# Forget sums of the keys: from TensorE products to rows read back from DRAM and added with the masks

## The chip, the core and the metric

The kernel runs on one core of one Trainium2 chip. Its engines are TensorE (PE, with its weight loads shown apart as PEld), VectorE (DVE), ScalarE (ACT), GpSimd (POOL) and SyncE (SP), which here only issues transfers. Times are device microseconds (us) of the whole program. Three runs of the kernel before took 1853.32, 1856.33 and 1856.56 us, so their median is 1856.33 us.

## The reference

One step of a two-layer network on 256 prompt rows and 8 streams of 16 sample rows (384 rows in all, three blocks of 128). Layer 0 has eight "fox" heads, softmax attention with a forget gate, and eight stick-breaking heads. Layer 1 is a gated MLP. The change touches the scores of the fox heads alone:

```python
F = cumsum(log_sigmoid(f_logit))                     # one forget sum per row and head
s = einsum('bqhd,bkhd->bhqk', q, k) * ATTN_SCALE
s = s + (Fq[..., :, None] - Fk[..., None, :])        # query's sum minus key's sum
s = where(kpos <= qpos, s, -inf)
p = softmax(s)
```

For a score matrix with queries on the partitions, `Fq` is one number per partition, and `-Fk` is one row that is the same for all partitions. The sample rows also attend to 128 cached keys per stream, whose sums run over the cached gates.

## The kernel before

All weights arrive in units of 256 KB (128 x 512 floats) that SP loads. Each unit is split into a rounded part `whi` (ACT, line 79) and a rest `wlo` (DVE, line 81); three products per block (lines 102 to 104, or 118 to 120) then give the result of one layer's projection in PSUM. `whi` and `wlo` have four buffers each, `raw` five, so a unit can be prepared about three units ahead of its use. The tiles named `d` are the PSUM banks of the projections (four), the tiles named `a` those of everything else (four).

Layer 0 starts with the transposes of x (line 162), then the keys of the first two heads (`first`), the row sums of squares (lines 204 and 207), their inverse root `rstd`, and `rstd_bc`, the same over all partitions, made by a product of a diagonal matrix `rdiag` with ones (line 147) and copied out by ACT (line 148). The values of the first heads come from `values_first` (lines 359 to 361), which also computes the forget logits.

`forget` then makes the sums. `FT` (8 heads x 384 rows) holds the sums of prompt and sample rows; `Fnat` holds the same with rows on partitions. The negated sums of the keys are kept in three tiles in the split form that TensorE's rounded type needs (heads on partitions 0 to 7 the rounded part, 32 to 39 the rest): `nFP` for prompt queries, `nFS` for the sample block, `nFc` for the cached keys. `E_all` picks one head out of these partitions for all 128 output partitions, and `selD` gives each group of 16 partitions its own stream's row.

`pair(g)` handles two heads. For g from 0 to 3 these are fox heads, for 4 to 7 stick-breaking heads. It projects keys, values, queries and gates, writes the keys back (`natural`), and loads the cached keys and values through POOL's queue (lines 420 and 422). `head` computes one head: `KT` by transposes on DVE (line 454), scores `sc` (prompt) and `sd` (sample) on TensorE, `z` = scores + `Fnat` + mask on DVE (line 481), the maximum, the exponential, and the products with the values.

The order of the instructions on each engine is fixed when the program is built: a scheduler runs the program text through a timing model and lets each engine take what that model says is ready. Every engine then works strictly in that order. A change of one instruction's modelled time can therefore move others.

Of the kernel before, what the change touches and what calls it, by code (L numbers as in the profile page):

```python
# [8 lines left out]
F32 = mybir.dt.float32  # L9
# [27 lines left out]
def tile_hybrid_step(  # L37
# [129 lines left out]
    with ExitStack() as l0:  # L167
# [44 lines left out]
        def late():  # L212
            es = ExitStack()
            for i in done[-1]:
                es.enter_context(tc.issue_after(i.ins))
            return es


        def select(ap, pattern, base, cm, fill=0.0, op=ALU.is_ge):
            G.affine_select(out=ap, in_=ap, pattern=pattern, compare_op=op, fill=fill, base=base, channel_multiplier=cm)  # L220
# [33 lines left out]
            select(mdn, [[-16, 8], [-1, 16]], -strict, 1, NEG)  # L254
            masks.append((mp, md))

        selD_f = lp.tile([P, P], F32, tag="os", name="selD_f")
        V.memset(selD_f, 0.0)
        sel8 = lp.tile([8, P], F32, tag="os", name="sel8")
        V.memset(sel8, 1.0)  # L260
        select(sel8, [[1, P]], 0, -16)
        select(sel8, [[-1, P]], 15, 16)
        selD = lc.tile([P, P], F32R, name="selD")
        with late():
            S.activation(selD_f[0:8], sel8, AF.Copy)
            S.activation(selD_f[32:40], sel8, AF.Copy)
            S.activation(selD, selD_f, AF.Copy)
        E_f = lc.tile([P, 8], F32, name="E_f")
        V.memset(E_f, 0.0)
        E_all = lc.tile([P, 8], F32R, name="E_all")  # L270
        with late():
            S.activation(E_f[0:8], ident[0:8, 0:8], AF.Copy)
            S.activation(E_f[32:40], ident[0:8, 0:8], AF.Copy)
            S.activation(E_all, E_f, AF.Copy)


        wf = lc.tile([P, KT, 8], F32, name="wf")
        bfg = lc.tile([P, 8], F32, name="bfg")
        clf = lc.tile([P, 8, 8], F32, name="clf")
        Fnat = lc.tile([P, NT, 8], F32, name="Fnat")  # L280
        nFP = lc.tile([P, T], F32R, name="nFP")
        nFS = lc.tile([P, T], F32R, name="nFS")
        nFc = lc.tile([P, 8, P], F32R, name="nFc")
        logf = lc.tile([P, NT, 8], F32, name="logf")

        V.tensor_copy(wf[:, 0, 0:1], hlo[1][:, 3, 0:1].bitcast(F32))
# [5 lines left out]
        def forget(o):  # L292
            gains(1)
            z = lc.tile([P, NT, 8], F32, name="fz")
            for tb in range(NT):
                V.scalar_tensor_tensor(out=z[:, tb, :], in0=o[tb][:, 256:264], scalar=rstd[:, tb:tb + 1], in1=bfg, op0=ALU.mult, op1=ALU.add)
            e = lc.tile([P, NT, 8], F32, name="fe")
            S.activation(e, z, AF.Abs)
            S.activation(e, e, AF.Exp, scale=-1.0)
            S.activation(e, e, AF.Ln, bias=1.0)  # L300
            V.scalar_tensor_tensor(out=logf, in0=z, scalar=0.0, in1=e, op0=ALU.min, op1=ALU.subtract)
            G.dma_start(flf_p.rearrange("o (t p) h -> p (o t) h", p=P), logf[:, :2, :])
            G.dma_start(flf_s.rearrange("b q h -> (b q) h"), logf[:, 2, :])

            b3 = bank()
            PE.matmul(b3[:8, :2 * P], lhsT=logf[:, 0, :], rhs=UT, start=True, stop=False)
            PE.matmul(b3[:8, P:2 * P], lhsT=logf[:, 1, :], rhs=UT[:, :P], start=False, stop=True)
            bs = bank()
            PE.matmul(bs[:8, :P], lhsT=logf[:, 2, :], rhs=BT, start=True, stop=True)
            for b_ in range(8):  # L310
                PE.matmul(bs[:8, P + b_:P + b_ + 1], lhsT=clf[:, b_, :], rhs=ones[:, 0:1], start=True, stop=True)
            tot = lc.tile([8, 8], F32, name="ftot")
            V.tensor_copy(tot, bs[:8, P:P + 8])
            FT = lp.tile([8, T], F32, tag="PT", name="FT")
            V.tensor_copy(FT[:, :2 * P], b3[:8, :2 * P])
            V.tensor_tensor(out=FT[:, 2 * P:].rearrange("h (b q) -> h b q", q=16), in0=bs[:8, :P].rearrange("h (b q) -> h b q", q=16),
                            in1=tot.unsqueeze(2).broadcast_to([8, 8, 16]), op=ALU.add)
            b4 = bank()
            for tb in range(NT):
                PE.transpose(b4[:, tb * 8:(tb + 1) * 8], FT[:, tb * P:(tb + 1) * P], ident[:8, :8])  # L320
            V.tensor_copy(Fnat, b4[:, :24].rearrange("p (t h) -> p t h", h=8))
            for t in (nFP, nFS):
                S.activation(t, ones[:, 0:1].broadcast_to([P, T]), AF.Copy, scale=0.0)
            for t, o, n, f in ((nFP, 0, 2 * P, 0), (nFP, 2 * P, P, 0), (nFS, 2 * P, P, 2 * P)):
                S.activation(t[0:8, o:o + n], FT[:, f:f + n], AF.Copy, scale=-1.0)
                V.scalar_tensor_tensor(out=t[32:40, o:o + n], in0=FT[:, f:f + n], scalar=-1.0, in1=f32(t[0:8, o:o + n]), op0=ALU.mult, op1=ALU.subtract)
            for hg in range(2):
                b5 = bank()
                for hh in range(4):
                    PE.matmul(b5[:8, hh * P:(hh + 1) * P], lhsT=clf[:, :, 4 * hg + hh], rhs=UT[:, :P], start=True, stop=True)  # L330
                hs = slice(4 * hg, 4 * hg + 4)
                b5v = b5[:8].rearrange("b (h p) -> b h p", p=P)
                S.activation(nFc[:, hs, :], ones[:, 0:1].unsqueeze(2).broadcast_to([P, 4, P]), AF.Copy, scale=0.0)
                S.activation(nFc[0:8, hs, :], b5v, AF.Copy, scale=-1.0)
                V.scalar_tensor_tensor(out=nFc[32:40, hs, :], in0=b5v, scalar=-1.0, in1=f32(nFc[0:8, hs, :]), op0=ALU.mult, op1=ALU.subtract)

        mixhi, mixlo = [], []
        vprev = [None]
# [108 lines left out]
        def head(g, hh, h, kT, vn, qT, kc, vc):  # L447
            fox = g < 4
            mp, md = masks[0 if fox else 1]

            KTt = []
            for hf in range(2):
# [2 lines left out]
                KTt.append(t)  # L455

            sc = bank()
            E_h = E_all[:, h:h + 1].broadcast_to([P, P])
            if fox:
                PE.matmul(sc[:, :T], lhsT=E_h, rhs=nFP, start=True, stop=False)  # L460
            PE.matmul(sc[:, :2 * P], lhsT=qT[:, P:2 * P], rhs=kT[:, :2 * P], start=not fox, stop=not fox)
            PE.matmul(sc[:, 2 * P:T], lhsT=qT[:, :P], rhs=kT[:, :P], start=not fox, stop=True)
            sd = bank()
            if fox:
                PE.matmul(sd[:, :T], lhsT=E_h, rhs=nFS, start=True, stop=False)
                PE.matmul(sd[:, :2 * P], lhsT=selD, rhs=nFc[:, h, :].unsqueeze(1).broadcast_to([P, 2, P]), start=False, stop=False)
# [307 lines left out]
```

## Time and profile before

| | |
|---|---|
| runs | 1853.32, 1856.33, 1856.56 us; median 1856.33 |
| profiled execution | 1854.33 us, of which the span from first to last instruction is 1852.6 us |
| granted TensorE clock | 0.998 of full speed |
| busy: PE, PEld, DVE, ACT, POOL | 99%, 90%, 52%, 39%, 12% of the span |
| DMA | 268 MB, mean 145 GB/s |

A row of a timeline gives the start in us, the time in us, engine, line, operation, the tile written and the tiles read, the shape, and how many instructions were merged. In brackets stands idle time of the engine just before the row, and what ended it. A PE matmul's end is modelled, and one starts while the one before it still drains, so what a matmul costs the engine is the distance from its start to the next one's start, not its duration.

### The profile page before, as it was taken

The page shows a single profiled execution, that of the slowest core. Times are in us where ns is not written, and L with a number is a line of the kernel's source. Part 1 is how long each engine was busy: PE and PEld are TensorE (multiplying, and loading weights), DVE is VectorE, ACT ScalarE, POOL GpSimd, SP SyncE. Part 2 cuts the span into 40 slices and gives each one's busy share as a digit, 9 for nine tenths or more (in the row PEclk, how much of TensorE's full clock was granted, in tenths as well). Part 3 has the DMA queues.
Part 4 walks back from the last instruction along what each step waited for, and adds up shares of the span by engine and source line. Part 5 has one row for each costly group of instructions (what it writes and reads, how often), then busy time and mean ns, then how long its engine had stood idle before and what let it go on. Part 6 is the DMA issues. An engine that isn't in the chain of part 4 may idle for free.

```text
span 1852.6 us, 27262 instructions
## 1 busy us (share of the span) xinstructions
PE 1828.7 (99%) x10107; PEld 1674.4 (90%) x10107; DVE 961.1 (52%) x1671; ACT 720.0 (39%) x1281; POOL 223.4 (12%) x366
## 2 busy tenths in 40 slices
PE   8999999999999999999999999999999999999997
PEld 7999899899899877788888999989998899989986
DVE  6555355556546544543343654545544555445456
ACT  5344343444544543433333433333332333333334
POOL 2421213213212001310000100001000100000000
PEclk9999999999999999999999999999999999999999
DMA  5855556565656467744444454445444444444453
GB/s 174 189 158 131 166 135 161 146 165 142 160 147 155 129 172 196 226 137 126 135 126 127 139 144 125 118 126 161 126 127 120 142 147 126 121 126 146 127 150 123
DMA packets 208582, 268.42 MB, mean 145 GB/s; under 512 B 19424, under 2 KB 149648, under 8 KB 208320
## 3 DMA queue, kind: packets, MB, share of 16 engines
q1 hardware_dynamic: 185088, 226.03, 43.3%
q0 software_dynamic: 16160, 35.93, 8.0%
q10 hardware_dynamic: 7200, 4.72, 0.8%
q8 instruction: 79, 1.29, 0.3%
q14 instruction: 55, 0.45, 0.1%
HBM read 251.91 MB, written 14.69 MB: 144 GB/s over the span
## 4 chain that ended last, share of the span: by engine, by line
PE 56%; DMA 3%; issue 2%; DVE 1%; ACT 1%; POOL 1%; ACTq 0%; POOLq 0%; DVEq 0%
PE d L104 9%; PE d L103 9%; PE d L102 9%; PE d L119 9%; PE d L120 9%; PE d L118 9%; DMA blk<-h1d 2%; PE a L673 1%; DMA raw<-in_w_out_dram 1%; POOL blk L553 0%; DMA slot<-in_sgu_ln_g_dram 0%; DMA h1d<-slot 0%; DVE wlo L81 0%; ACT sq L722 0%; DVE slot L719 0%
## 5 line engine op out<-in xcount | busy, mean ns | idle before, releaser
L81 DVE TENSOR_TENSOR wlo<-raw,whi 128x512 fp32r<-128x512 f32 x800 | 547.3, 690 | 716.1 <-ACT whi L79 715.0
L79 ACT ACTIVATE whi<-raw 128x512 fp32r<-128x512 f32 x800 | 503.5, 631 | 930.5 <-PE d L103 492.3
L104 PE MATMUL d<-slot,wlo 128*128 128x384 f32 x1792 | 601.7, 337 | 0.6 <-DVE wlo L81 0.6
L102 PE MATMUL d<-slot,whi 128*128 128x384 f32 x1792 | 601.5, 336 | 0.0
L103 PE MATMUL d<-slot,whi 128*128 128x384 f32 x1792 | 601.2, 335 | 0.0
L119 PE MATMUL d<-wlo,slot 128*128 128x512 f32 x1056 | 410.1, 391 | 4.3 <-DVE wlo L81 4.3
L120 PE MATMUL d<-whi,slot 128*128 128x512 f32 x1056 | 408.1, 390 | 0.0
L118 PE MATMUL d<-whi,slot 128*128 128x512 f32 x1056 | 371.2, 391 | 0.3 <-DVE slot L573 0.3
L104 PEld LDWEIGHTS d<-slot,wlo 128*128 128x128 f32 x1792 | 336.3, 188 | 7.4 <-issue 6.4
L102 PEld LDWEIGHTS d<-slot,whi 128*128 128x128 f32 x1792 | 336.9, 188 | 0.5
L103 PEld LDWEIGHTS d<-slot,whi 128*128 128x128 f32 x1792 | 336.9, 188 | 0.4
L119 PEld LDWEIGHTS d<-wlo,slot 128*128 128x128 f32 x1056 | 198.3, 188 | 46.6 <-DVE wlo L81 6.0
L118 PEld LDWEIGHTS d<-whi,slot 128*128 128x128 f32 x1056 | 198.1, 188 | 42.1 <-DVE slot L573 0.8
L120 PEld LDWEIGHTS d<-whi,slot 128*128 128x128 f32 x1056 | 198.2, 188 | 40.8
L647 POOL DMA_DIRECT2D wr<-in_w_sp_dram x64 | 34.8, 551 | 407.0 <-DVE wT L651 407.0
L393 POOL DMA_DIRECT2D out_dram<-knat x64 | 38.0, 594 | 126.0 <-DVE knat L387 125.7
L640 DVE TENSOR_TENSOR slot<-d,slot 128x512 f32<-128x512 f32 x48 | 32.6, 688 | 15.7 <-PE d L120 15.6
L394 POOL DMA_DIRECT2D out_dram<-knat x64 | 36.0, 562 | 0.0
L553 POOL DMA_DIRECT2D blk<-h1d x16 | 14.6, 919 | 159.0 <-DMA h1d<-slot 158.8
L420 POOL DMA_DIRECT2D kcache<-in_cache_sb_k_dram x32 | 25.0, 787 | 71.9 <-DVE KT L454 57.6
L420 POOL DMA_DIRECT2D kcache<-in_cache_fox_k_dram x32 | 25.2, 793 | 64.1 <-DVE st L482 44.8
L601 POOL TENSOR_SCALAR rsv<-mvr 128x3 f32<-128x3 f32 x1 | 0.5, 543 | 223.2 <-DVE mvr L600 223.2
(230 smaller groups left out, 1184.3 us busy)
## 6 DMA issues: line engine op xcount, KB each, us to landing
raw<-in_w_in_dram SPq DMA_DIRECT2D x640, 256.0 KB, 2.8
raw<-in_w_out_dram SPq DMA_DIRECT2D x192, 256.0 KB, 3.1
kcache<-in_cache_fox_k_dram POOLq DMA_DIRECT2D x32, 128.0 KB, 5.5
vcache<-in_cache_fox_v_dram POOLq DMA_DIRECT2D x4, 1024.0 KB, 7.1
kcache<-in_cache_sb_k_dram POOLq DMA_DIRECT2D x32, 128.0 KB, 5.9
vcache<-in_cache_sb_v_dram POOLq DMA_DIRECT2D x4, 1024.0 KB, 6.2
h1d<-slot ACTq DMA_DIRECT2D x12, 256.0 KB, 2.4
blk<-h1d POOLq DMA_DIRECT2D x16, 192.0 KB, 8.0
```

What stands on the lines that cost most here:

```text
L79: S.activation(hi, raw, AF.Copy)
L81: V.tensor_tensor(out=lo, in0=raw, in1=f32(hi), op=ALU.subtract)
L102: PE.matmul(o, lhsT=hi[:, kk, cs], rhs=h, start=(k == 0), stop=False)
L103: PE.matmul(o, lhsT=hi[:, kk, cs], rhs=l, start=False, stop=False)
L104: PE.matmul(o, lhsT=lo[:, kk, cs], rhs=h, start=False, stop=(k == KT - 1))
L118: PE.matmul(o, lhsT=his[k][:, t], rhs=hi[:, 0, :], start=(k == 0), stop=False)
L119: PE.matmul(o, lhsT=his[k][:, t], rhs=lo[:, 0, :], start=False, stop=False)
L120: PE.matmul(o, lhsT=los[k][:, t], rhs=hi[:, 0, :], start=False, stop=(k == nk - 1))
L393: G.dma_start(o_p[:, h0 + hh, :, js], nat[js, hh, :8, :])
L394: G.dma_start(o_s[:, h0 + hh, :, js], nat[js, hh, 8:, :])
L420: G.dma_start(kcache[32 * j:32 * j + 32, hh, :].rearrange("p (b d) -> p b d", d=32), kc[:, :, h0 + hh, 32 * j:32 * j + 32].rearrange("b (i ...
L647: G.dma_start(wr[js, 0, :].rearrange("p (a s) -> p a s", s=32), w_sp[g, :, js].rearrange("(a p) s -> p a s", p=32))
```

## The change

The tiles `selD`, `E_all`, `nFP`, `nFS` and `nFc` and all that made them go. Two DRAM tensors take their place: `nFd` (8 heads x 384 sums) and `nFcd` (8 streams x 8 heads x 128 sums). `forget` negates `FT` once on DVE and writes it to `nFd` by POOL's queue, and ACT copies the two halves of the cached sums, which are written to `nFcd`. Each fox head then issues four loads on POOL's queue that spread a row over all partitions (512 bytes or 1 KB to each of the 128 partitions), adds the masks on POOL into a tile `fb` (three additions of 384, 128 and 256 columns; `fb` has two buffers, the tile `fc` of the cached sums one), and line 481 takes `fb` where it took the mask. The three products per fox head with `E_all` and `selD` go.

```diff
-        nFP = lc.tile([P, T], F32R, name="nFP")
-        nFS = lc.tile([P, T], F32R, name="nFS")
-        nFc = lc.tile([P, 8, P], F32R, name="nFc")
+        nFd = dram.tile([8, T], F32, name="nFd")
+        nFcd = dram.tile([8, 8, P], F32, name="nFcd")
...
-            for t in (nFP, nFS):
-                S.activation(t, ones[:, 0:1].broadcast_to([P, T]), AF.Copy, scale=0.0)
...
+            nFT = lp.tile([8, T], F32, tag="PT", name="nFT")
+            V.tensor_scalar(out=nFT, in0=FT, scalar1=-1.0, scalar2=None, op0=ALU.mult)
+            G.dma_start(nFd, nFT)
...
+                nFc = lp.tile([8, 4, P], F32, tag="KT", name=nm("nFc"))
+                S.activation(nFc, b5v, AF.Copy, scale=-1.0)
+                G.dma_start(nFcd[:, hs, :], nFc)
...
+            if fox:
+                fb = lp.tile([P, 2, T], F32, tag="fb", name=nm("fb"))
+                fc = lp.tile([P, P], F32, tag="fc", bufs=1, name=nm("fc"))
+                G.dma_start(fb[:, 0, :2 * P], nFd[h, :2 * P].partition_broadcast(P))
+                G.dma_start(fb[:, 0, 2 * P:], nFd[h, :P].partition_broadcast(P))
+                G.dma_start(fb[:, 1, 2 * P:], nFd[h, 2 * P:].partition_broadcast(P))
+                G.dma_start(fc, nFcd[:, h, :].unsqueeze(1).broadcast_to([8, 16, P]))
+                G.tensor_tensor(out=fb[:, 0, :], in0=fb[:, 0, :], in1=mp, op=ALU.add)
+                G.tensor_tensor(out=fb[:, 1, 2 * P:], in0=fb[:, 1, 2 * P:], in1=md[:, 2 * P:], op=ALU.add)
+                G.tensor_tensor(out=fb[:, 1, :2 * P].rearrange("p (s k) -> p s k", s=2), in0=md[:, :2 * P].rearrange("p (s k) -> p s k", s=2),
+                                in1=fc.unsqueeze(1).broadcast_to([P, 2, P]), op=ALU.add)
+                mp, md = fb[:, 0, :], fb[:, 1, :]
...
-            if fox:
-                PE.matmul(sc[:, :T], lhsT=E_h, rhs=nFP, start=True, stop=False)
...
-                PE.matmul(sd[:, :T], lhsT=E_h, rhs=nFS, start=True, stop=False)
-                PE.matmul(sd[:, :2 * P], lhsT=selD, rhs=nFc[:, h, :].unsqueeze(1).broadcast_to([P, 2, P]), start=False, stop=False)
```

The scheduler moves other work with it. On PE, in the startup, the product that makes `rstd_bc` (`a_400<-rdiag`) stands among the products of the first values (`d_512`, `d_513`, `d_514`: three row blocks). Before:

```order
L360 MATMUL d_513<-wlo_596,slot_154 128x264
L361 MATMUL d_513<-whi_595,slot_155 128x264
L359 MATMUL d_513<-whi_595,slot_154 128x264
L360 MATMUL d_513<-wlo_596,slot_154 128x264
L147 MATMUL a_400<-rdiag_396,ones 128x384 [waits DVE_49,PE_49]
L361 MATMUL d_513<-whi_595,slot_155 128x264
L176 MATMUL a_728<-ident,graw 128x16 [waits DMASW2_49,PE_49]
L359 MATMUL d_514<-whi_517,slot_128 128x264 [waits DVE_49]
```

And with the change, where the lines are those of the new text (338 to 340 are 359 to 361) and the blocks are called `d_495` to `d_497`:

```order
L340 MATMUL d_495<-whi_578,slot_155 128x264
L147 MATMUL a_400<-rdiag_396,ones 128x384 [waits DVE_49,PE_49]
L338 MATMUL d_495<-whi_578,slot_154 128x264
L339 MATMUL d_495<-wlo_579,slot_154 128x264
L340 MATMUL d_495<-whi_578,slot_155 128x264
L338 MATMUL d_496<-whi_578,slot_154 128x264
L339 MATMUL d_496<-wlo_579,slot_154 128x264
L340 MATMUL d_496<-whi_578,slot_155 128x264
L338 MATMUL d_496<-whi_578,slot_154 128x264
L339 MATMUL d_496<-wlo_579,slot_154 128x264
L340 MATMUL d_496<-whi_578,slot_155 128x264
L176 MATMUL a_711<-ident,graw 128x16 [waits DMASW2_49,PE_49]
```

Between `L147` and `L176` stand nine products where there was one: the product for `rstd_bc` moved eight places ahead.

On PE, the three products per fox head are gone and nothing took their place. In the very first head alone, the products with the cached keys (line 469, now 455) stand some 60 places behind the other scores' (now 450 to 453), not right after them, and its softmax moves back too.

On DVE, around the first head's `z` before:

```order
L81 TENSOR_TENSOR wlo_1147<-raw_1143,whi_1145 128x512
L81 TENSOR_TENSOR wlo_1165<-raw_1161,whi_1163 128x512
L481 SCALAR_TENSOR_TENSOR z_965<-a_953,Fnat,mp_417 128x256
L481 SCALAR_TENSOR_TENSOR z_965<-a_953,Fnat,mp_417 128x128
L482 TENSOR_REDUCE st_966<-z_965 128x1
L481 SCALAR_TENSOR_TENSOR z_983<-a_957,Fnat,md_425 128x384
```

And with the change, from the unit on that follows the second of the two above (446 is the old 454, 360 the old 381, 467 the old 481; `KT_936` and `KT_938` are the first head's transposes, `KT_1011` and `KT_1013` the second's):

```order
L81 TENSOR_TENSOR wlo_1173<-raw_1169,whi_1171 128x512
L81 TENSOR_TENSOR wlo_1191<-raw_1187,whi_1189 128x512
L81 TENSOR_TENSOR wlo_1209<-raw_1205,whi_1207 128x512
L446 STREAM_TRANSPOSE KT_936<-kcache_471 128x512
L446 STREAM_TRANSPOSE KT_938<-kcache_471 128x512
L81 TENSOR_TENSOR wlo_1249<-raw_1245,whi_1247 128x512
L81 TENSOR_TENSOR wlo_1267<-raw_1263,whi_1265 128x512
L446 STREAM_TRANSPOSE KT_1011<-kcache_471 128x512
L446 STREAM_TRANSPOSE KT_1013<-kcache_471 128x512
L81 TENSOR_TENSOR wlo_1285<-raw_1281,whi_1283 128x512
L360 TENSOR_TENSOR gz_1223<-d_1077,rstd_bc 128x384
L467 SCALAR_TENSOR_TENSOR z_949<-a_940,Fnat,fb_927 128x256
```

The first head's `z` stands six weight units later than before, behind the transposes for both heads.

On POOL, after the change, the first two heads' `fb` tiles (`fb_927` and `fb_1002`), their cached sums (`fc_928`, `fc_1003`), the next pair's cached keys (`kcache_1241`) and the third head's `fb_1769`, from the write of the cached sums on; line 399 is the old 420:

```order
L436 DMA fc_928<-nFcd 128x1x128 [waits DMASW2_49]
L437 TENSOR_TENSOR fb_927<-fb_927,mp_417 128x384 [waits DMASW5_49,DMASW4_49]
L438 TENSOR_TENSOR fb_927<-fb_927,md_425 128x128 [waits DMASW6_49]
L437 TENSOR_TENSOR fb_1002<-fb_1002,mp_417 128x384 [waits DMASW7_49,DMASW0_49]
L399 DMA kcache_1241<-in_cache_fox_k_dram 32x32x32 [waits DMASW3_49,DVE_49]
L399 DMA kcache_1241<-in_cache_fox_k_dram 32x32x32 x5
L399 DMA kcache_1241<-in_cache_fox_k_dram 32x32x32 [waits DMASW1_49]
L399 DMA kcache_1241<-in_cache_fox_k_dram 32x32x32 [waits DMASW2_49]
L438 TENSOR_TENSOR fb_1002<-fb_1002,md_425 128x128
L439 TENSOR_TENSOR fb_927<-md_425,fc_928 128x256
L436 DMA fc_1003<-nFcd 128x1x128 [waits DMASW3_49,Pool_49]
L433 DMA fb_1769<-nFd 128x256 [waits DMASW4_49,DVE_49]
```

The last addition for the first head (`fb_927<-md_425,fc_928`) stands behind the eight loads of cached keys, which themselves wait for DVE; before the change these eight loads had nothing of a head behind them.

## Rows read from the trace of the kernel before

**Rows 1.** Part 1 of the page: busy time, share of the span, instructions.
```profile
PE 1828.7 (99%) x10107; PEld 1674.4 (90%) x10107; DVE 961.1 (52%) x1671; ACT 720.0 (39%) x1281; POOL 223.4 (12%) x366
```

**Rows 2.** Part 5 of the page: groups, busy and mean ns, idle before.
```profile
L81 DVE TENSOR_TENSOR wlo<-raw,whi 128x512 fp32r<-128x512 f32 x800 | 547.3, 690 | 716.1 <-ACT whi L79 715.0
L79 ACT ACTIVATE whi<-raw 128x512 fp32r<-128x512 f32 x800 | 503.5, 631 | 930.5 <-PE d L103 492.3
L104 PE MATMUL d<-slot,wlo 128*128 128x384 f32 x1792 | 601.7, 337 | 0.6 <-DVE wlo L81 0.6
```

**Rows 3.** Timeline of PE in the first fox head.
```profile
74.06 0.34 PE L460 MATMUL a<-nFP,E_all 128*128 128x384 f32 x1
74.24 0.34 PE L465 MATMUL a<-nFS,E_all 128*128 128x384 f32 x1
74.41 0.28 PE L466 MATMUL a<-nFc,selD 128*128 128x256 f32 x1
74.53 0.34 PE L102 MATMUL d<-slot,whi 128*128 128x384 f32 x1
```

**Rows 4.** Timeline of PE, a second fox head, then a second stick-breaking head.
```profile
92.69 0.38 PE L530 MATMUL a<-PT,vnat 128*128 128x128 f32 x2
...
94.35 0.64 PE L469 MATMUL a<-KT,qT 128*32 128x256 f32 x8
...
418.84 0.38 PE L530 MATMUL a<-PT,vnat 128*128 128x128 f32 x2
...
420.03 0.64 PE L469 MATMUL a<-KT,qT 128*32 128x256 f32 x8
```

**Rows 5.** Timeline of PE in the startup, around line 147.
```profile
38.62 0.28 PE L361 MATMUL d<-whi,slot 128*128 128x264 f32 x1
...
39.60 0.81 PE L147 MATMUL a<-rdiag,ones 128*128 128x384 f32 x2
39.95 0.58 PE L361 MATMUL d<-whi,slot 128*128 128x264 f32 x1
...
41.58 0.39 PE L359 MATMUL d<-whi,slot 128*128 128x264 f32 x1 [0.89 <-DVE kT L381]
```

**Rows 6.** Timeline of ACT in the startup.
```profile
27.92 0.29 ACT L265 ACTIVATE selD_f<-sel 8x128 f32<-8x128 f32 x1
...
29.01 0.63 ACT L204 ACTIVATE sq<-slot 128x512 f32<-128x512 f32 x1
...
40.44 0.49 ACT L148 ACTIVATE rstd_bc<-a 128x384 f32<-128x384 f32 x1 [4.83 <-PE a L147]
```

**Rows 7.** Timeline of DVE, startup and around the first fox head.
```profile
40.97 1.02 DVE L381 TENSOR_TENSOR kT<-d,rstd_bc 128x384 f32<-128x384 f32 x2
...
77.31 0.69 DVE L81 TENSOR_TENSOR wlo<-raw,whi 128x512 fp32r<-128x512 f32 x1 [1.86 <-ACT whi L79]
...
81.69 0.68 DVE L81 TENSOR_TENSOR wlo<-raw,whi 128x512 fp32r<-128x512 f32 x1
...
87.33 0.69 DVE L81 TENSOR_TENSOR wlo<-raw,whi 128x512 fp32r<-128x512 f32 x1 [1.39 <-ACT whi L79]
```

**Rows 8.** Groups by line on POOL, whole span.
```profile
L607 POOL DMA_DIRECT2D slot<-in_sgu_ln_g_dram x8 | 4.5, 563 | 163.2 <-ACT whi L79 163.2
L140 POOL TENSOR_TENSOR rstd<-tot,ex 128x3 f32<-128x3 f32 x2 | 2.3, 1152 | 0.2
L220 POOL TENSOR_SCALAR_AFFINE_SELECT md<-md 128x128 f32<-128x128 f32 x6 | 1.9, 335 | 0.0
```

**Rows 9.** Timeline of POOL around the first fox head.
```profile
62.17 0.92 POOL L422 DMA_DIRECT2D vcache<-in_cache_fox_v_dram  x1
81.65 6.37 POOL L420 DMA_DIRECT2D kcache<-in_cache_fox_k_dram  x8 [18.56 <-DVE KT L454]
```

**Rows 10.** DMA issues: count, KB each, median us from issue to landing.
```profile
vcache<-in_cache_fox_v_dram POOLq DMA_DIRECT2D x4, 1024.0 KB, 7.1
slot<-in_sgu_ln_g_dram POOLq DMA_DIRECT2D x8, 256.0 KB, 5.8
```

More of the change, by code (lines that the diff above doesn't have):

```diff
@@ L255, in tile_hybrid_step @@
             masks.append((mp, md))
[L257 to L274, printed above, removed]
         wf = lc.tile([P, KT, 8], F32, name="wf")
@@ L321, in forget @@
             V.tensor_copy(Fnat, b4[:, :24].rearrange("p (t h) -> p t h", h=8))
-            for t in (nFP, nFS):
-                S.activation(t, ones[:, 0:1].broadcast_to([P, T]), AF.Copy, scale=0.0)
-            for t, o, n, f in ((nFP, 0, 2 * P, 0), (nFP, 2 * P, P, 0), (nFS, 2 * P, P, 2 * P)):
-                S.activation(t[0:8, o:o + n], FT[:, f:f + n], AF.Copy, scale=-1.0)
-                V.scalar_tensor_tensor(out=t[32:40, o:o + n], in0=FT[:, f:f + n], scalar=-1.0, in1=f32(t[0:8, o:o + n]), op0=ALU.mult, op1=ALU.subtract)
+            nFT = lp.tile([8, T], F32, tag="PT", name="nFT")
+            V.tensor_scalar(out=nFT, in0=FT, scalar1=-1.0, scalar2=None, op0=ALU.mult)
+            G.dma_start(nFd, nFT)
             for hg in range(2):
@@ L332, in forget @@
                 b5v = b5[:8].rearrange("b (h p) -> b h p", p=P)
-                S.activation(nFc[:, hs, :], ones[:, 0:1].unsqueeze(2).broadcast_to([P, 4, P]), AF.Copy, scale=0.0)
-                S.activation(nFc[0:8, hs, :], b5v, AF.Copy, scale=-1.0)
-                V.scalar_tensor_tensor(out=nFc[32:40, hs, :], in0=b5v, scalar=-1.0, in1=f32(nFc[0:8, hs, :]), op0=ALU.mult, op1=ALU.subtract)
+                nFc = lp.tile([8, 4, P], F32, tag="KT", name=nm("nFc"))
+                S.activation(nFc, b5v, AF.Copy, scale=-1.0)
+                G.dma_start(nFcd[:, hs, :], nFc)
         mixhi, mixlo = [], []
@@ L457, in head @@
             sc = bank()
-            E_h = E_all[:, h:h + 1].broadcast_to([P, P])
-            if fox:
-                PE.matmul(sc[:, :T], lhsT=E_h, rhs=nFP, start=True, stop=False)
-            PE.matmul(sc[:, :2 * P], lhsT=qT[:, P:2 * P], rhs=kT[:, :2 * P], start=not fox, stop=not fox)
-            PE.matmul(sc[:, 2 * P:T], lhsT=qT[:, :P], rhs=kT[:, :P], start=not fox, stop=True)
+            PE.matmul(sc[:, :2 * P], lhsT=qT[:, P:2 * P], rhs=kT[:, :2 * P], start=True, stop=True)
+            PE.matmul(sc[:, 2 * P:T], lhsT=qT[:, :P], rhs=kT[:, :P], start=True, stop=True)
             sd = bank()
-            if fox:
-                PE.matmul(sd[:, :T], lhsT=E_h, rhs=nFS, start=True, stop=False)
-                PE.matmul(sd[:, :2 * P], lhsT=selD, rhs=nFc[:, h, :].unsqueeze(1).broadcast_to([P, 2, P]), start=False, stop=False)
-            PE.matmul(sd[:, 2 * P:T], lhsT=qT[:, 2 * P:T], rhs=kT[:, 2 * P:T], start=not fox, stop=not fox)
+            PE.matmul(sd[:, 2 * P:T], lhsT=qT[:, 2 * P:T], rhs=kT[:, 2 * P:T], start=True, stop=True)
             for j in range(4):
                 PE.matmul(sd[32 * j:32 * j + 32, :2 * P], lhsT=qT[:, 2 * P + 32 * j:2 * P + 32 * j + 32], rhs=KTt[j // 2][:, (j % 2) * 256:(j % 2) * 256 + 256],
-                          start=not fox, stop=True)
+                          start=True, stop=True)
             PTs = []
```

## The prediction, before the changed kernel ran

> **What bounds the kernel now.** I read the busy shares first, then the groups by line for what ends each engine's idle time, then the timelines of PE, DVE, ACT and POOL where the change touches them. PE is busy 99% of the span, POOL 12% [rows 1]. The groups say who waits for whom: ACT's `whi` waits for PE to give a buffer back, DVE's `wlo` waits for ACT, and PE in its turn lost 0.6 us to `wlo` over 1792 products [rows 2]. So PE sets the pace from about 42 us on, and DVE, ACT and POOL are worth time only where they make PE wait. Matmuls overlap, so I price them by distances between starts.
>
> How far DVE runs ahead of PE decides what a late score costs. A unit has 12 products that start 0.17 to 0.18 us apart [rows 3]; on DVE one unit is 0.69 us of work behind 1.39 us of waiting, 2.08 us in all [rows 7]. `whi` for a unit begins when PE frees the fourth buffer, that is with three units before it, 6.24 us; ACT takes 0.63 and DVE 0.69 of that [rows 2], so `wlo` is ready 4.9 us early. Around the first fox head two `wlo` stand 4.38 us apart instead of 2.08 [rows 7], so a head's own DVE work already uses 2.3 of the 4.9; 2.6 us are left there.
>
> **The change part by part.**
>
> *Products removed.* In the first head of each pair the three products stand together, and the next start comes 74.53 - 74.06 = 0.47 us later [rows 3]. In the second head they stand between others; there a fox head takes 94.35 - 92.69 = 1.66 us from line 530 to line 469, and a stick-breaking head, which has the same products without these three, 420.03 - 418.84 = 1.19 us [rows 4]. The difference is 0.47 us again. Eight heads: 8 x 0.47 = 3.8 us, all of it on the engine that sets the end.
>
> *Startup.* ACT loses the copies for `selD` and `E_all`; the first four took 29.01 - 27.92 = 1.09 us between the squares [rows 6], and the squares end the chain to `rstd`. The scheduler answers by moving line 147 eight products ahead on PE. Before, PE waited there: `rstd_bc` waits for line 147, DVE's first `kT` for `rstd_bc`, and PE stood 0.89 us for `kT` (it frees the bank of the third row block) before 41.58 [rows 5 to 7]. Eight products start from 38.62 on before line 147 does at 39.60, so it would start 0.98 us earlier; it showed no wait of its own before, and its inputs now come 1.09 us earlier, so they should be there. `rstd_bc` then starts near 39.46 instead of 40.44 [rows 6] and ends 0.49 us later, the first half of `kT` (0.51 of 1.02 us) ends near 40.5, and PE resumes near 40.6 instead of 41.58: 1.0 us. It is nothing if the bank is late for another reason, and not over 1.1 us, the whole of the wait and what surrounds it. I take 1.0, the value that the rows give step by step.
>
> *Regrouping.* In the first head alone the old compact group is cut into two, and its transposes into two. Each time PE goes from weights' products to a head's and back it loses something: after line 466 nothing shows [rows 3], while line 147, a full-width product set among `values_first`, takes 0.35 us to the next start [rows 5] where a product of its width takes 0.17 [rows 3]: 0.18 lost. Three more such changes are bounded by 0 below and 0.55 us above; I take 0.3, the middle, since no row is nearer.
>
> *Work taken from ACT and DVE.* The fills, splits and memsets were hidden: DVE's `wlo` waits 1.39 us of each 2.08 for ACT, ACT waits for PE [rows 2, 7]. Zero, startup aside. `nFT` and the negated `nFc` cost less than what they replace.
>
> *POOL's new work.* Per head four loads and three additions. A load that spreads a row over the partitions exists already: 0.563 us to issue [rows 8], 5.8 us to land for 256 KB [rows 10]. No addition over 384 columns is in the trace; below, 128 columns of a select take 0.335 us, so 768 columns in three pieces 2.0 us; above, I add to this 1.15 us for each instruction, what a POOL tensor operation on only three columns took [rows 8]: 5.5 us. I take 2.5, near the select, since line 140 is a power and not an addition. [...] With 2.3 us of issues and my 2.5 POOL gets 4.8 us a head, 38 us in all (34 to 62 by the two ends), on an engine idle 88% of the time. What it costs is decided by when `fb` is needed.
>
> *The round trip of the first head.* POOL is through with the cached values' issue at 63.1 [rows 9]; the write of `nFd` follows, and if it lands only behind those values it lands about 62.17 + 7.1 = 69.3 [rows 9, 10], say 70. The six loads of the first two heads take 3.4 us to issue, the first head's own two land by 70 + 1.1 + 5.8 = 77, and line 437's addition ends near 78.5. In the new DVE order `z` stands behind six more `wlo` than the one at 77.31, so at 77.31 + 6 x 2.08 = 89.8, about 89 with the startup's gain. Margin 10 us. The second half of the first head's mask stands on POOL behind eight loads of cached keys, 6.37 us [rows 9], released by DVE's transposes for the second head; DVE has eight `wlo` (16.6 us) between these transposes and the `z` that wants it. Margin 9 us after an addition of about 1 us. The next addition, for the second head, stands behind loads into `fb` that wait for that `z`; four `wlo` (8.3 us) lie before its use and it needs about 3. Behind a waiting `z` on DVE stand the `wlo` that PE wants, which is why the margins matter; all three are positive, so I cost this at nothing. If the cover went, each us beyond margin plus 2.6 would be a us of PE. For the third head the load stands already behind the second's on POOL, a whole pair ahead of its use, and so on.
>
> *Traffic.* Each head reads 128 x 2.5 KB, 0.33 MB; eight heads 2.6 MB of 268. `raw` has five buffers, 10 us ahead at 2.08 us a unit. Zero.
>
> Sum: -3.8 - 1.0 + 0.3 = -4.5 us; 1854.33 - 4.5 = 1849.8 for an execution like the profiled one. That one lies 2.0 below the median of 1856.33, so on the median I predict 1851.8. What a measurement can tell from no change is 0.2%, 3.7 us, so this is a gain just beyond it.
>
> **The rivals.**
>
> 1. *Less is gained than I add up*: the startup's 1.0 us comes back elsewhere (PE arrives earlier at the same bank, or at `whi` made by ACT) and regrouping costs its 0.55. For: other small stalls stand close by, and the regrouping is bounded, not measured. Against: PE's 0.89 us wait has one clear releaser [rows 5]. -3.8 + 0.6 = -3.2: 1853.1 (-0.17%), within 0.2%.
>
> 2. *POOL's reading and DVE's reading shut each other out.* A `wlo` cannot then start while a POOL addition runs. Nothing in the trace shows or excludes it: no POOL operation before reads 384 columns beside DVE. The three additions of a head, if back to back on the upper bound of 5.5 us, would exceed the 2.6 us left around a head by 2.9; in four of eight heads 11.6 us: 1856.3 - 4.5 + 11.6 = 1863.4, slower. With 2.0 to 2.5 us of additions the 2.6 covers it and only the forecast remains. [...] By the order the additions mostly stand away from the heads' dense DVE stretches, which speaks against a loss.
>
> 3. *The first `z` waits for POOL.* The round trip through DRAM in the busiest stretch takes not 15 us but over 28. Then DVE stands at `z`, `wlo` behind it, and PE runs dry. It decides from 89 + 2.6 = 91.6 on; to make the kernel slower by 3.7 us `fb` must be ready past 100. With landings three times those of the rows (`nFd` at 62.17 + 21.3 = 84 with the rest, `fb` at 84 + 1.1 + 17.4 + 1.5 = 104) it would lose 12.4 us: 1864.2. For: POOL's queue works in order and writes and reads wait for each other. Against: the rows of landings are medians of transfers far larger than these.
>
> **How the numbers follow.** Forecast 0.56. Rival 1 0.28. Rival 2 0.08, of which half lands near no change and half slower. Rival 3 0.06. Something I did not see 0.02, slower. Faster by over 0.2%: 0.56. Within 0.2%: 0.28 + 0.04 = 0.32. Slower: 0.04 + 0.06 + 0.02 = 0.12. The forecast's own range is -3.0 to -5.2 with the scatter of the runs before, 1853.32 to 1856.56, around it: 1848 to 1853.5. To hold 8 in 10 the range reaches over rival 1 and part of rival 2: 1847.5 to 1857.0.
>
> **What would show it.** The profile after should show: 24 PE products fewer and PE's count of lines 450 to 455 otherwise the same; the first and second heads in 1.19 us where they are compact; line 147 near 38.6 and no wait for `kT` behind it; line 467's `z` with no idle time that POOL ended; `wlo` still waiting for ACT alone, and the groups of products with no more idle time to `wlo` than 0.6 us. It is wrong if a `z` waits for POOL by over 2.6 us, if `wlo` grows well past 0.69 us while POOL adds, or if PE shows new gaps between 60 and 330 us.

## The result, and the profile after

The changed kernel took 1843.39 us, median of six runs (1842.85 to 1844.90). The kernel before, run beside it, took 1854.49 (six runs, 1852.40 to 1856.56). The ratio is 0.994, its 95% interval 0.9927 to 0.9953: faster, by 11.1 us. The forecast was 1851.8 us, range 1847.5 to 1857.0, a gain of 4.5 us. The sign is right, the size is not.

The profiled execution has a span of 1841.5 us at a granted clock of 0.999. Part 1 of the page after, answering to [rows 1]:

```profile
PE 1823.2 (99%) x10083; PEld 1669.7 (91%) x10083; DVE 966.6 (52%) x1664; ACT 715.6 (39%) x1268; POOL 262.0 (14%) x423
```

The 24 products are gone, POOL works 38.6 us more. The groups by line of after, answering to [rows 2 and 8], with POOL's additions and `z` below:

```profile
L81 DVE TENSOR_TENSOR wlo<-raw,whi 128x512 fp32r<-128x512 f32 x800 | 553.1, 697 | 715.6 <-ACT whi L79 714.3
L104 PE MATMUL d<-slot,wlo 128*128 128x384 f32 x1792 | 601.0, 336 | 0.3 <-DVE wlo L81 0.3
L119 PE MATMUL d<-wlo,slot 128*128 128x512 f32 x1056 | 409.7, 390 | 0.3 <-DVE wlo L81 0.3
L437 POOL TENSOR_TENSOR fb<-fb,mp 128x384 f32<-128x384 f32 x8 | 8.7, 1090 | 10.2 <-DMA fb<-nFd 10.2
L439 POOL TENSOR_TENSOR fb<-md,fc 128x256 f32<-128x256 f32 x8 | 6.1, 760 | 3.7 <-DMA fc<-nFcd 3.7
L438 POOL TENSOR_TENSOR fb<-fb,md 128x128 f32<-128x128 f32 x8 | 5.4, 680 | 0.1
L467 DVE SCALAR_TENSOR_TENSOR z<-a,Fnat,fb 128x256 f32<-128x256 f32 (+2 forms) x24 | 10.6, 469 | 7.4 <-PE a L451 7.4
```

The three additions take 2.5 us a head, as forecast, and DVE never sat idle before a `z` because of POOL. The row to look at is L119, the products of the units that are 512 columns wide. In the kernel before it reads:

```profile
L119 PE MATMUL d<-wlo,slot 128*128 128x512 f32 x1056 | 410.1, 391 | 4.3 <-DVE wlo L81 4.3
```

PE stood 4.3 us for `wlo` there, 0.3 us after. That stood in the list of groups before, and the prediction read only its neighbour L104 with 0.6.

The startup, PE after, answering to [rows 5], then DVE's first `kT` [rows 7]:

```profile
37.49 0.81 PE L147 MATMUL a<-rdiag,ones 128*128 128x384 f32 x2
...
39.32 0.23 PE L176 MATMUL a<-ident,graw 16*128 16x16 f32 x1
39.48 0.39 PE L338 MATMUL d<-whi,slot 128*128 128x264 f32 x1
```

```profile
38.86 1.02 DVE L360 TENSOR_TENSOR kT<-d,rstd_bc 128x384 f32<-128x384 f32 x2 [4.03 <-ACT rstd_bc L148]
```

The product that waited 0.89 us before starts with no wait. The first fox head, PE after, answering to [rows 3]:

```profile
75.42 0.59 PE L450 MATMUL a<-kT,qT 128*128 128x256 f32 x2
75.86 0.38 PE L451 MATMUL a<-kT,qT 128*128 128x128 f32 x2
76.08 0.39 PE L453 MATMUL a<-kT,qT 128*128 128x128 f32 x2
76.22 0.42 PE L104 MATMUL d<-slot,wlo 128*128 128x384 f32 x1
...
86.63 0.63 PE L455 MATMUL a<-KT,qT 128*32 128x256 f32 x4
...
87.56 0.63 PE L455 MATMUL a<-KT,qT 128*32 128x256 f32 x4
```

The three products are gone, and the head's eight products with the cached keys (line 455) come 10 us behind its other scores, in two groups of four: this is the regrouping that the forecast spoke of.

The round trip, POOL after [rows 9], then DVE in the same stretch:

```profile
60.84 0.56 POOL L305 DMA_DIRECT2D nFd<-nFT  x1
...
68.95 0.57 POOL L433 DMA_DIRECT2D fb<-nFd  x1 [3.61 <-DMA nFd<-nFT]
...
74.57 1.01 POOL L437 TENSOR_TENSOR fb<-fb,mp 128x384 f32<-128x384 f32 x1 [1.75 <-DMA fb<-nFd]
```

```profile
74.73 1.41 DVE L81 TENSOR_TENSOR wlo<-raw,whi 128x512 fp32r<-128x512 f32 x1 [1.39 <-ACT whi L79]
...
91.15 0.74 DVE L467 SCALAR_TENSOR_TENSOR z<-a,Fnat,fb 128x256 f32<-128x256 f32 x2
```

`fb` is ready at 75.6, `z` wants it at 91.2: a margin of 15 us where 10 were forecast. The `wlo` that meets the additions at 74.57 and 75.56 takes 1.41 us instead of 0.69. No `wlo` of the kernel before took over 0.70 us, and in the changed kernel each one that took over 0.82 stood beside an addition, so I put the longer time down to POOL's additions. Ten more `wlo` that met an addition took 0.94 to 1.56 us; beside two others, at 163.4 and 165.5 us, `wlo` kept its 0.69 us and the addition took longer (1.55 instead of 1.0 us the first). A longer `wlo` is one of the forecast's signs of being wrong, but it cost nothing: PE waits for no engine between 74 and 340 us.

**Where the time went.** I laid the starts of the same TensorE products of two traces side by side and noted by how much the difference to the kernel before changes across a stretch (bounds on the clock of before, us gained negative). The first row is the changed kernel, the others are the experiments below, each against the one trace of before; between 60 and 74 us nothing changes:

| kernel | 0-37 | 37-60 | 74-340 (fox heads) | 340-640 | 640-790 (output projection) | 790-end |
|---|---|---|---|---|---|---|
| changed kernel | -1.14 | -0.96 | -3.56 | -0.48 | **-5.01** | -0.13 |
| h1d moved | -0.61 | 0 | 0 | 0 | +0.05 | +0.07 |
| after, h1d back | +0.86 | -0.96 | -3.55 | -0.49 | -5.44 | -0.56 |
| after, zero products | -0.03 | -0.96 | +0.38 | -0.52 | -5.26 | 0 |
| before, no products | -1.28 | 0 | -3.82 | 0 | -1.06 | +0.4 |
| before, blk aligned | -0.24 | 0 | 0 | -0.06 | -5.18 | +0.7 |
| after, blk misaligned | -0.28 | -0.96 | -3.40 | -0.33 | -1.90 | -1.0 |
| before, all aligned | +0.17 | 0 | 0 | -0.35 | -5.59 | -0.6 |
| before, 35 transfers | +1.11 | +0.16 | 0 | 0 | +1.02 | +0.9 |
| after, additions x4 | -0.05 | -0.96 | +3.64 | -0.49 | -5.57 | +0.5 |
| before, no products, no copies | -0.41 | -0.96 | -3.83 | 0 | -2.98 | +0.5 |
| after, blk at offset 32 | -0.04 | -0.96 | -3.40 | -0.33 | -2.85 | +0.2 |

The two stretches that the forecast spoke of give -0.96 - 3.56 = -4.5 us, its sum (in part by luck, as the account of the prediction says below). Another 5.0 us came from 640 to 790 us, hundreds of us behind the change, where not one instruction is added, removed or moved. The chain of waits in that stretch, before, and below it after (start, us, what):

```profile
668.53 10.39 DMA blk<-h1d
...
700.26 8.83 DMA blk<-h1d
...
733.82 9.04 DMA blk<-h1d
...
767.75 9.45 DMA blk<-h1d
```

```profile
724.90 8.49 DMA blk<-h1d
```

There h1 goes to DRAM and comes back transposed in pieces of 32 floats (`blk`). DVE stands in its queue for `blk`, 24.4 us over the four turns, the `wlo` behind it come late, and PE waits 4.3 us for them. The tile view of `blk`, who sat idle for it and its landing times, before and then after:

```profile
  DMA blk<-h1d: 24.4, 4
...
DMA to landing us min/median/max: 4.8/8.0/10.4
```

```profile
  DMA blk<-h1d: 16.7, 4
...
DMA to landing us min/median/max: 4.0/7.0/8.5
```

DVE's wait fell from 24.4 to 16.7 us over the four turns. The question for the experiments was why the same reads land sooner.

### The profile page after: what moved, and what is told of

Its sections match the earlier page's. It is cut to its first block, busy times and chain, and to the rows that moved or that the text cites. A ratio compares the mean times of both kernels' runs of the same rounds, so it can differ in the third digit from the quotient of the medians.

```text
span 1841.5 us, 27281 instructions
## 1 busy us (share of the span) xinstructions
PE 1823.2 (99%) x10083; PEld 1669.7 (91%) x10083; DVE 966.6 (52%) x1664; ACT 715.6 (39%) x1268; POOL 262.0 (14%) x423
## 4 chain that ended last, share of the span: by engine, by line
PE 95%; DMA 2%; issue 1%; DVE 1%; ACT 1%; POOL 0%; SPq 0%; ACTq 0%; POOLq 0%; DVEq 0%
PE d L104 17%; PE d L103 17%; PE d L102 17%; PE d L118 12%; PE d L119 12%; PE d L120 12%; PE a L659 1%; DMA raw<-in_w_out_dram 1%; PE d L338 1%; PE d L339 1%; PE d L340 1%; PE a L495 1%; PE a L515 1%; PE a L455 1%; DMA blk<-h1d 0%
## 5 line engine op out<-in xcount | busy, mean ns | idle before, releaser
L81 DVE TENSOR_TENSOR wlo<-raw,whi 128x512 fp32r<-128x512 f32 x800 | 553.1, 697 | 715.6 <-ACT whi L79 714.3
L104 PE MATMUL d<-slot,wlo 128*128 128x384 f32 x1792 | 601.0, 336 | 0.3 <-DVE wlo L81 0.3
L119 PE MATMUL d<-wlo,slot 128*128 128x512 f32 x1056 | 409.7, 390 | 0.3 <-DVE wlo L81 0.3
L104 PEld LDWEIGHTS d<-slot,wlo 128*128 128x128 f32 x1792 | 336.1, 188 | 6.6 <-issue 6.0
L119 PEld LDWEIGHTS d<-wlo,slot 128*128 128x128 f32 x1056 | 198.3, 188 | 41.3 <-DVE wlo L81 0.7
L593 POOL DMA_DIRECT2D slot<-in_sgu_ln_g_dram x8 | 4.5, 564 | 163.2 <-ACT whi L79 163.2
```

The source lines that it names most:

```text
L81: V.tensor_tensor(out=lo, in0=raw, in1=f32(hi), op=ALU.subtract)
L104: PE.matmul(o, lhsT=lo[:, kk, cs], rhs=h, start=False, stop=(k == KT - 1))
L119: PE.matmul(o, lhsT=his[k][:, t], rhs=lo[:, 0, :], start=False, stop=False)
```

## The experiments

Each was timed beside the kernel before, whose medians were 1854.2 to 1854.7 us.

**Where h1d lies, and what the products are worth.** The change puts two tiles ahead of `h1d` in DRAM, which moves it by 45056 bytes. Moved alone:

```diff
+        pad = dram.tile([11, 1024], F32, name="pad")
+        G.dma_start(pad[0:1, 0:4], ones[0:1, 0:4])
```

> The kernel before, with one more DRAM tile of 44 KB (16 bytes of it are written early by POOL) so that h1d lies at the same offset in DRAM as in the changed kernel. Open is why the four turns of the output projection (640 to 790 us of the kernel before) lost 5.0 us. Place in DRAM: the reads blk<-h1d land in a median of 7.0 us instead of 8.0, and the time is 1849.5 (-5.0). Place in SBUF, or the phase of the loads against each other: blk stays at 8.0 and the time at 1854.5 (0).

Measured: 1853.82, ratio 1.0 (0.9992 to 1.0009), `blk` 7.9 us. And back, in the changed kernel:

```diff
+        hd = dram.tile([4 * 4 * T * P + 8 * T + 64 * P], F32, name="hd")
...
+        h1d = hd[:4 * 4 * T * P].rearrange("(c k t d) -> c k t d", c=4, k=4, t=T)
```

> The changed kernel with h1d back at the DRAM offset of the kernel before (the sums lie behind it in the same tile). Place in DRAM: blk<-h1d back to a median near 8.0 us, time 1848.4 (+5.0 on the changed kernel, -6.1 on before). Place in SBUF or phase of the loads: 1843.4 (-11.1 on before), blk 7.0.

Measured: 1843.69, ratio 0.9943 (0.993 to 0.9955), `blk` 6.8 us. The place in DRAM is out.

Products back into the changed kernel, with a zero weight tile `zr`:

```diff
+                PE.matmul(sc[:, :T], lhsT=zr, rhs=hk(hhi, 0), start=True, stop=False)
...
+                PE.matmul(sd[:, :T], lhsT=zr, rhs=hk(hhi, 0), start=True, stop=False)
+                PE.matmul(sd[:, :2 * P], lhsT=zr, rhs=hk(hhi, 0)[:, :2 * P], start=False, stop=False)
```

> The changed kernel with the 24 removed products put back as products with a zero weight tile (they add nothing to the scores; same columns, same groups). Price of the products alone, as forecast (3.8 less 0.3): 1846.9 (+3.5 on the changed kernel, -7.6 on before), and the four turns keep their 5.0 us. If the turns gain only because they come 3 to 6 us earlier against the loads (phase), they may fall back as well: up to 1852 (+8.5).

Measured: 1847.83, ratio 0.9966 (0.9954 to 0.9979): +4.4 on the changed kernel. The fox heads' stretch goes from -3.56 to +0.38, so the products are worth 3.9 us there. The four turns keep their gain (-5.26), although they come 5.0 us later than in the changed kernel.

Products out of the kernel before:

```diff
-                PE.matmul(sc[:, :T], lhsT=E_h, rhs=nFP, start=True, stop=False)
...
-                PE.matmul(sd[:, :T], lhsT=E_h, rhs=nFS, start=True, stop=False)
-                PE.matmul(sd[:, :2 * P], lhsT=selD, rhs=nFc[:, h, :].unsqueeze(1).broadcast_to([P, 2, P]), start=False, stop=False)
```

> The kernel before without the 24 products (it leaves out the keys' forget sums from the scores; all tiles, copies and the masks as before). Price of the products alone: 1851.0 (-3.5), blk<-h1d at a median of 8.0 us as before. Phase: the turns gain as in the changed kernel, 1846.0 (-8.5), blk 7.0. Places in DRAM or SBUF: 1851.0.

Measured: 1847.52, ratio 0.9962 (0.9949 to 0.9976), 3.5 more than the price of the products. By the table the fox heads gave 3.82 us, 3.8 as forecast; 1.28 lies before 37 us, where nothing of this edit is, and only 1.06 in the turns, `blk` 7.7 us. Arriving 5 us earlier (this kernel) does not bring the gain of the turns, arriving 1 us earlier (zero products) does not lose it: the phase of the loads does not explain the 5.0 us. It may explain the 1.06.

In this kernel the first head's eight products with the cached keys stand together, so nothing is regrouped:

```profile
77.23 0.64 PE L463 MATMUL a<-KT,qT 128*32 128x256 f32 x8
```

That gives a price for the regrouping. Split at 154 us, just ahead of the second pair's scores, the column of the fox heads falls into -0.94 and -2.88 here, -0.45 and -3.11 in the changed kernel. With the zero products, which are regrouped like the changed kernel, it is +0.53 and -0.15. So the regrouped kernels lose 0.5 us in the first pair, and nothing in the other three, where POOL adds for six of the eight heads.

**Where blk lies in SBUF.** The kernels whose turns gain little (h1d moved, no products) have the SBUF layout of before, the others that of the changed kernel. The change removes tiles that lie ahead of `kcache`, whose place `blk` takes over. In the compiled program it begins at byte 177472 of each partition before, 64 past a multiple of 128, and at 168704 after, a multiple of 128. Only this undone, in the kernel before (`fz` and `fe` move into KT's place to make room for the pads):

```diff
+        lc.tile([P, 16], F32, name="pl")
...
+                lp.tile([P, 16], F32, tag="pk", bufs=1, name="pk")
             kcache = lp.tile([P, 2, 8 * P], F32, tag="kcache", bufs=1, name=nm("kcache"))
+                lp.tile([P, 16], F32, tag="pv", bufs=1, name="pv")
```

> The kernel before, where only kcache (whose place blk takes) lies on another SBUF address: 177408 bytes instead of 177472, a multiple of 128 bytes as in the changed kernel; vcache and all behind it stay, what lies ahead of kcache moves by 128 bytes. The transfers into blk and kcache write pieces of 128 bytes. Alignment of blk: blk<-h1d lands in a median of 7.0 instead of 8.0 us, the four turns gain 5.0 us, time 1849.5. Another cause (number of POOL's transfers): blk 8.0, 1854.5.

Measured: 1848.61, ratio 0.9969 (0.9958 to 0.9981): -5.7 us from 64 bytes. The turns give -5.18, `blk` 7.3 us. Groups by line, L119:

```profile
L119 PE MATMUL d<-wlo,slot 128*128 128x512 f32 x1056 | 409.8, 390 | 0.0
```

The last two pads alone, in the changed kernel, where their effect is the reverse:

```diff
+                lp.tile([P, 16], F32, tag="pk", bufs=1, name="pk")
...
+                lp.tile([P, 16], F32, tag="pv", bufs=1, name="pv")
```

> The changed kernel with kcache and blk 64 bytes further up in SBUF (off the multiple of 128), and all behind by 128. Alignment of blk: blk<-h1d back to 8.0 us, time 1848.4 (+5.0 on the changed kernel, -6.1 on before). Another cause: 1843.4 (-11.1 on before).

Measured: 1848.10, ratio 0.9969 (0.9957 to 0.998): +4.7 on the changed kernel. PE waits for `wlo` again (its waits from 640 to 790 us: total, times, longest):

```profile
PE d L119 <- DVE wlo L81: 2.7, 3, 1.5
```

All tiles of the pool aligned, by moving `fz` and `fe` alone:

```diff
-            z = lc.tile([P, NT, 8], F32, name="fz")
+            z = lp.tile([P, NT, 8], F32, tag="KT", name="fz")
```

> The kernel before with all tiles of layer 0's working pool 192 bytes lower (two small tiles of the forget gate share the place of KT), so that all of them begin on a multiple of 128 bytes, not kcache alone. Alignment: 1849.5 for blk, and another 0.5 less (1849.0) if the loss between 340 and 640 us, which the changed kernel has and the runs with the tiles of before do not, hangs on other tiles than kcache. Another cause: 1854.5.

Measured: 1848.44, ratio 0.9968 (0.9955 to 0.998), -5.9. The extra 0.5 cannot be told in the times; in the trace 340 to 640 us gives -0.35, so that small loss belongs to tiles other than `kcache`. Which ones stays open.

The rival, the number of POOL's transfers:

```diff
+            if fox:
+                pads(4)
```

> The kernel before with 35 more transfers of 16 bytes on POOL's queue at the places where the changed kernel issues its 35 (three behind the forget gate, four in each of the eight heads). Number and order of POOL's transfers: blk 7.0 us, 1849.5 (-5.0). Alignment of blk: 8.0 us, 1854.5 (0).

Measured: 1857.36, ratio 1.0015 (1.0006 to 1.0024), `blk` 8.1 us. The number is out. It cost 3.0 us instead of nothing: 1.1 before 37 us, 1.0 in the turns, 0.9 behind them. The scheduler put line 147 one product later and PE's wait for `kT` grew from 0.89 to 1.01 us, but that is only 0.1 us; the rest is not explained.

One more offset in the changed kernel, 32 bytes instead of 64:

```diff
+                lp.tile([P, 8], F32, tag="pk", bufs=1, name="pk")
...
+                lp.tile([P, 24], F32, tag="pv", bufs=1, name="pv")
```

> The changed kernel with kcache and blk 32 bytes further up in SBUF, where the earlier run had 64; all behind lies as in that run. If any place off a multiple of 128 bytes makes the 128-byte pieces slow: 1848.1 (+4.7 on the changed kernel, as at 64 bytes), POOL's queue at 8.9% of the 16 engines. If 64 bytes is a special case: 1843.4, POOL's queue at 8.2%.

Measured: 1847.29, ratio 0.996 (0.9947 to 0.9974): +3.9 on the changed kernel, `blk` 7.6 us. How long the packets of POOL's queue took says it without any wait in between. Part 3 of the page (packets, MB, share of 16 engines' span), in this order: before, before with blk aligned, changed kernel, changed with offset 64, with offset 32:

```profile
q0 software_dynamic: 16160, 35.93, 8.0%
```

```profile
q0 software_dynamic: 16160, 35.93, 7.4%
```

```profile
q0 software_dynamic: 17536, 38.60, 8.2%
```

```profile
q0 software_dynamic: 17536, 38.60, 8.9%
```

```profile
q0 software_dynamic: 17536, 38.60, 8.9%
```

Same packets, same bytes; the queue takes 8 to 9% more time off the multiple of 128. Over all kernels the turns gave -5.0 to -5.6 us with `blk` on a multiple of 128 (six kernels), and -3.0 to +1.0 off it (six, beside the kernel before). PE's waits for `wlo` in the turns are 0.3 us at most in the first six. Off the multiple they are 3.7 to 4.4 us in the three kernels that reach the turns no earlier than before (before itself, h1d moved, 35 transfers), and 1.5 to 3.2 in the four that reach them about 5 us earlier. So in these kernels the waits are gone on a multiple of 128 whenever PE arrives; off it their size varies, and an earlier arrival seems to take a part. In the kernel before the alignment alone brings the whole gain. In the changed kernel, which arrives 6 us earlier, 1.9 and 2.9 us of it remain when the alignment is undone.

**The startup.** The six copies taken out as well:

```diff
-            S.activation(selD_f[0:8], sel8, AF.Copy)
-            S.activation(selD_f[32:40], sel8, AF.Copy)
-            S.activation(selD, selD_f, AF.Copy)
...
-            S.activation(E_f[0:8], ident[0:8, 0:8], AF.Copy)
-            S.activation(E_f[32:40], ident[0:8, 0:8], AF.Copy)
-            S.activation(E_all, E_f, AF.Copy)
```

> The kernel before without the 24 products (as in the earlier run) and also without the six ACT copies that make selD and E_all, which then have no reader (tiles stay in place; the forget sums of the keys are left out of the scores). Startup term: line 147 stands eight products further ahead on TensorE, the products of the first value block come 0.96 us earlier, 1846.6 (-0.96 on the run without products, 1847.5). If the startup's gain came from something else in the change (the missing fills of nFP, nFS and nFc, or the transfers), 1847.5.

Measured: 1847.17, ratio 0.9964 (0.9951 to 0.9976), -0.35 on the run without products alone, which the times cannot tell from either expectation. The traces can. PE without products, then without products and copies:

```profile
38.32 0.81 PE L147 MATMUL a<-rdiag,ones 128*128 128x384 f32 x2
...
40.30 0.39 PE L359 MATMUL d<-whi,slot 128*128 128x264 f32 x1 [0.89 <-DVE kT L381]
```

```profile
38.23 0.81 PE L147 MATMUL a<-rdiag,ones 128*128 128x384 f32 x2
...
40.05 0.23 PE L176 MATMUL a<-ident,graw 16*128 16x16 f32 x1
40.21 0.39 PE L351 MATMUL d<-whi,slot 128*128 128x264 f32 x1
```

Line 147 goes eight products ahead, the wait for `kT` is gone, and 37 to 60 us gives -0.96, the very number of the changed kernel: the copies are the whole cause of it.

**POOL against DVE.** The additions four times over:

```diff
+                for _ in range(4):
+                    G.tensor_tensor(out=fb[:, 0, :], in0=fb[:, 0, :], in1=mp, op=ALU.add)
...
```

> The changed kernel with POOL's three additions of each of the eight heads done four times over (masked places get a larger negative number, the result stays). Hidden work, with the 0.3 us that the runs so far leave for all of POOL's new work: three more sets cost 3 x 0.3 = 0.9 us at most, 1844.3 (+0.9), no z waits for POOL (each set is 2.4 us, the margin of the first head about 15 us). [...]

(The 0.3 us from which this starts lies in the first pair alone, so it fits the regrouping and not POOL's work, see above.) Measured: 1851.29, ratio 0.9984 (0.9975 to 0.9993): +7.9 on the changed kernel. That is more than the 0.9 of hidden work, and far less than if DVE lost the time of every addition put in, 58 us by an estimate from 2.4 us a set (8 x 3 x 2.4). The fox heads' stretch lost 7.2 us. PE's waits there, 74 to 345 us, of which the changed kernel has none, then DVE, then POOL, in the first pair:

```profile
PE a L514 <- DVE os L511: 3.4, 1, 3.4
PE d L104 <- DVE wlo L81: 2.8, 2, 2.3
```


```profile
95.16 1.50 DVE L81 TENSOR_TENSOR wlo<-raw,whi 128x512 fp32r<-128x512 f32 x1 [1.68 <-ACT whi L79]
96.58 7.81 DVE L412 SCALAR_TENSOR_TENSOR sg<-gz,sg 128x768 f32<-128x768 f32 x1
```

```profile
96.61 0.48 POOL L439 TENSOR_TENSOR fb<-fb,md 128x128 f32<-128x128 f32 x1
97.03 0.74 POOL L440 TENSOR_TENSOR fb<-md,fc 128x256 f32<-128x256 f32 x1
...
102.58 0.98 POOL L438 TENSOR_TENSOR fb<-fb,mp 128x384 f32<-128x384 f32 x1
103.54 1.16 POOL L439 TENSOR_TENSOR fb<-fb,md 128x128 f32<-128x128 f32 x1
```

The `sg` of line 412 takes 0.96 us elsewhere (the median of the eight is 0.958) and 7.81 here, beside eleven additions of a row of 13; in the second pair a `gz` of line 414 took 9.05 us beside a row of twelve. PE's waits stand right behind these two. But the length of a row does not decide alone. In the next row, of ten, a `wlo` lost only 0.2 us and an addition waited for it (1.46 instead of 1.01 us):

```profile
139.02 0.87 DVE L81 TENSOR_TENSOR wlo<-raw,whi 128x512 fp32r<-128x512 f32 x1 [1.73 <-ACT whi L79]
```

```profile
139.30 1.46 POOL L438 TENSOR_TENSOR fb<-fb,mp 128x384 f32<-128x384 f32 x1
```

So in these two kernels DVE's operations did take longer beside POOL's additions (up to 1.56 us instead of 0.69, and up to 9.05 instead of 0.96), as rival 2 supposed, and the price was not proportional to the additions. That it is the reading of the two that shuts them out is not shown. Both operations that lost 7 and 8 us met rows of twelve and more, all other rows being of ten at most; why DVE lost so much in these two and 0.2 us in the next is not shown.

No run points to a version that would beat the changed kernel: in it all tiles that receive pieces of 128 bytes already begin on a multiple of 128.

## Why the prediction was wrong in size

- *Products removed*: forecast -3.8; the two kernels without products and without POOL's new work give -3.82 and -3.83. Right.
- *Startup*: forecast -1.0, measured -0.96 in all seven kernels without the copies and in none with them. Right, mechanism too.
- *Regrouping*: forecast +0.3 between bounds of 0 and 0.55. The first pair of heads, the only one that is regrouped, loses 0.5 us in the kernels that are regrouped, against the kernel before without products, which is not. Right in kind, a little small. POOL's first additions and the later softmax fall into the same pair, so this is its most likely cause and not one tested alone.
- *POOL's new work*: forecast 0. In the other three pairs, which hold six of the eight heads' additions, the changed kernel loses nothing against the kernel without products; it gains 0.2 us, and no run says why. This 0.2 makes up for what the regrouping cost beyond 0.3, so that the sum of the heads came out exactly is luck.
- *Round trip*: margin 10 forecast, 15 measured; `nFd` landed 7.8 us after its issue, at 68.6, where 70 was forecast. The second half of the first mask was added by 96.8 and wanted at 105.1, a margin of 8 where 9 were forecast. Right.
- *Rival 2*: what it supposed of DVE came about in part (eleven of the `wlo` beside an addition took 0.94 to 1.56 us, two kept 0.69), its loss did not. In the changed kernel two additions at most stand in a row, and no operation of DVE lost more than 1.3 us (an `mx` of line 420), less than the 2.6 us of slack around a head that the forecast set against it.
- **The step that failed** is *Traffic ... Zero*, with the sentence that PE loses 0.6 us to `wlo` in 1792 products [rows 2]. It counted the bytes that the change adds and did not ask what the transfers that stay would cost on other addresses, and it read L104's idle time and not L119's 4.3 us in the same list. The removed tiles moved `blk` by 8768 bytes onto a multiple of 128, its reads land in 7.0 instead of 8.0 us, and PE's stalls in the four turns go: -5.0 in the trace. In the times it is -5.7 and -5.9 in the two kernels that align `blk` and change nothing else of weight, and +4.7 and +3.9 in the two that undo it in the changed kernel; the traces of these last two show only +3.1 and +2.2 in the turns.
- What is left: 0.5 us between 340 and 640 us, tied to the layout by the kernel with all aligned, tile not found; and 1.1 us before 37 us. The latter scatters from -1.28 to +0.86 between traces of kernels that start alike, so I take it for the arrival of x and not for the change, without having shown it. Lastly the forecast was set on a median of three runs (1856.33) that later runs of the kernel before put at 1854.5: another 1.8 us.

So the 8.4 us between forecast and result are about 5.5 that go with the layout, 1.8 from the base, 1.1 from the start.

## What to carry to other kernels

A change that adds or removes a tile moves every tile allocated behind it: before pricing it, find the transfers with small pieces that land behind it, and look whether their start crosses from on to off a multiple of 128 bytes (here 64 and 32 bytes off it cost 4.7 and 3.9 us). Read all groups that PE waits in, not only those next to the change; a wait of 4.3 us anywhere is something that an unrelated edit can give back or take. Additions on POOL beside VectorE were cheap in ones and twos (no operation lost over 1.3 us), and could be dear in a long row (two operations lost 7 and 8 us).

## What the runs showed of the hardware

Pieces of 128 bytes written to SBUF cost POOL's queue 8 to 9% more of its time when the tile begins 32 or 64 bytes past a multiple of 128 (8.0 against 7.4%, 8.9 against 8.2% of the engines' span). Offsets of 32 and 64 bytes gave the same 8.9%. An odd multiple of 128 did as well as an even one: in the kernel with all aligned `blk` begins at 177472 - 192 = 177280, which is 1385 x 128, and its turns gained 5.59 us; in the kernel with `blk` alone aligned it begins at 177408, which is 1386 x 128, and they gained 5.18; POOL's queue took 7.3% and 7.4%. Why the queue takes longer off the multiple is not shown.

Two VectorE operations that met a row of POOL additions, a `sg` of line 412 and a `gz` of line 414, took 7.81 and 9.05 us instead of 0.96, beside eleven and twelve additions of which none took over 1.2 us; beside the next row, of ten, a `wlo` took 0.87 us instead of 0.69. In the changed kernel a `wlo` beside two additions, of 1.01 and 0.90 us, took 1.41 us instead of 0.69, one beside a single addition of 1.03 us took 1.56, and one beside an addition of 1.55 us kept its 0.69.
